# Seven products on three PSUM banks, a down projection that finishes token tile by token tile, and new homes for two kinds of tiles

## The chip, the cores and the metric

The kernel runs on one core of one Trainium2 chip. The metric is the device time of one execution in microseconds (us), as the median of several runs. TensorE (PE) does the matmuls, VectorE (DVE), ScalarE (ACT) and GpSimd (POOL) do the elementwise work, and SyncE (SP) issues every DMA of this kernel, all on one queue, in program order.

## The reference

One layer of a hybrid decoder on 2048 tokens of width 1024, in fp32: a norm, an input projection with three mixers (two gated linear attentions and a linear recurrence), an output projection with a residual, and then a gated feed-forward part with a final norm. The change touches only the feed-forward part, whose inner width is 2688, 21 channels of 128 (`NFF`):

```
h = rmsnorm(x, norm_ffn[l])
gate = causal_dwconv(h @ ffn_w_gate[l], ffn_conv_w[l], ffn_conv_b[l])
x = x + (jax.nn.gelu(gate) * (h @ ffn_w_val[l])) @ ffn_w_down[l]
...
return rmsnorm(x, norm_final)
```

`causal_dwconv` is a convolution over three tokens for each column.

## The kernel before, in words

**fp32 by parts.** Every matmul operand is split into a high and a low fp32r part: ACT copies (`wh`, `gh`: line 100), DVE subtracts (`wl`, `gl`: line 107). A product is then three matmuls, high by high, high by low, low by high (lines 130 to 132 and 992).

**Stages.** Mixers and output projection come first (0 to 975 us); they are not touched. Then two halves of 1024 tokens (`TH`) follow one another, each with an up stage and a down stage: up 0 (975 to 1379 us), down 0 (to 1636), up 1 (to 2027.4), down 1 (to 2261.6), and a tail without matmuls.

**Up** (`up`). For each channel f the gate and the value projection of 1024 tokens (two blocks of 512, `TB`) are computed with seven products of half matrices in place of eight, in Strassen's manner: the weights enter as `x`, `y`, `z`, `w` (sums and differences of the gate's and the value's weights, split by `w_steps`), the tokens as `b1`, `t12`, `t34`, `b22`. A product is 12 matmuls of 512 columns, so a channel is 84. Their sums go to four PSUM banks (`ca` and `cd` of the mm banks, `cb` aux, `cc` sc); ACT and DVE add them up into `gr` (the gate before the convolution), `u` (a partial sum that several results share) and `v` (the value). Then come convolution (`ga`), gelu and `v = ga * v`, which is stored as channel f of `g_ffn` in DRAM (line 1025). Channels use two tile pools in turn, `f_up0` for even and `f_up1` for odd f. The last channel, f = 20, is even.

**Down** (`down`). Token tiles of 128 go in groups, (3, 3, 2) tiles in down 0 and (4, 4) in down 1. A group loads its residuals `xr` (512 KB each, line 1038) and runs over the 21 channels: it loads a row block of `w_down` (`wr`, 512 KB, split into `wh`, `wl`; 3 buffers), loads `graw`, the gated activations of the channel and the group's tokens (192 KB for 3 tiles, 256 KB for 4; 4 buffers, line 1042), splits it into `gh`, `gl` (3 buffers), and adds six matmuls for each tile. After the last channel every tile gets its residual, the final norm and one store of 512 KB. Down 0 also prepares the second half's tokens (`h_steps`: norm, transposes on PE, sums) beside its channels.

**What sets the order.** A scheduler orders the instructions of each engine by priority and by when their buffers come free. Each engine then runs its list strictly in order and stops at a wait, SP too. Pools that follow one another take the same addresses: the down stage's pools `f_g` (`graw`, `gh`, `gl`) and `f_o` (`nfb`, `xr`) lie where `f_up0` and `f_up1` lay. A load into a place must wait until the last reader of that place is done; if that reader was a store, until the store has landed.

**Where the tiles lie** (addresses in a partition). Before: `f_up1` lies 8192 bytes below the top of the up stage's space and so leaves a pad at 191680 to 199872. `graw`'s four buffers fill exactly that pad, which no up tile uses, and all of `f_g` ends at 212160, below `f_up0`. `xr` overlaps the `v` of the last channel.

Of the kernel before, what the change touches and what calls it, by code (L numbers as in the profile page):

```python
# [8 lines left out]
F32 = mybir.dt.float32  # L9
F32R = mybir.dt.float32r  # L10
I32 = mybir.dt.int32
AF = mybir.ActivationFunctionType
ALU = mybir.AluOpType
# [3 lines left out]
P = 128  # L17
D = 1024
KT = D // P
TB = 512  # L20
NTK = TB // P
EPS = 1e-6
# [21 lines left out]
def kernel(ctx: ExitStack, tc: tile.TileContext, x, norm_mix, w_in, hgrn_lower_bounds, hgrn_norm,  # L44
# [10 lines left out]
    def pool_at(stack, nbytes, name, bufs, **kw):  # L55

        stack.enter_context(tc.tile_pool(name="pad_" + name, bufs=1, **kw)).tile([P, nbytes // 4], F32, name="pad")
        return stack.enter_context(tc.tile_pool(name=name, bufs=bufs, **kw))
# [21 lines left out]
    def mm_bank():  # L80
        return bank("mm", 4)

    def aux_bank():
        return bank("aux", 2)

    def sc_bank():
        return bank("sc", 2)
# [16 lines left out]
    def split(raw, hi, lo, e_hi=act, e_lo=vec):  # L104

        copy(e_hi, hi, raw)
        e_lo.tensor_tensor(lo, raw, hi.bitcast(F32), op=ALU.subtract)  # L107
# [20 lines left out]
    def mm3(o, lhs, rhs, first, last):  # L128
        (lh, ll), (rh, rl) = lhs, rhs
        pe.matmul(o, lh, rh, start=first, stop=False)  # L130
        pe.matmul(o, lh, rl, start=False, stop=False)  # L131
        pe.matmul(o, ll, rh, start=False, stop=last)  # L132

    def rms_rstd(src, n):
        junk = junk_t().bitcast(mybir.dt.bfloat16)
        ss = small.tile([P, 1], F32, name="ss")
        act.activation(junk, src, AF.Square, accum_out=ss)
        r = small.tile([P, 1], F32, name="rstd")
        vec.tensor_scalar(r, ss, 1.0 / n, EPS, op0=ALU.mult, op1=ALU.add)  # L139
        pool.tensor_tensor(r, r, half, op=ALU.pow)  # L140
        return r
# [567 lines left out]
    with ExitStack() as cy:  # L709
# [165 lines left out]

        junk_t = lambda: stage.tile([P, TB], F32, name="junk", tag="st")
        hc = cy.enter_context(tc.tile_pool(name="f_hc", bufs=1, reuse_waits="tile"))
        fc = cy.enter_context(tc.tile_pool(name="f_const", bufs=1, reuse_waits="tile"))  # L880
# [95 lines left out]
        def up(hf, H, pools):  # L976

            nextw, steps = w_steps(0)
            for st in steps:
                st()  # L980
            for f in range(NFF):
                W, pool_ = nextw, pools[f % 2]
                if f + 1 < NFF:
                    nextw, steps = w_steps(f + 1)
                else:
                    steps = [lambda: None] * 5

                def prod(o, w, wk, h, hk, first, last):
                    for k in range(KH):
                        lhs, rhs = [a[:, wk + k, :] for a in w], [a[:, hk + k, :] for a in h]  # L990
                        for i, (a, b) in enumerate(((0, 0), (0, 1), (1, 0))):
                            pe.matmul(o, lhs[a], rhs[b], start=first and k == 0 and i == 0, stop=k == KH - 1 and i == 2,  # L992
                                      skip_group_check=True)
                gr = pool_.tile([P, 2 + TH], F32, name="gr")
                ga = pool_.tile([P, TH], F32, name="ga")
                v = pool_.tile([P, TH], F32, name="v")
                u = pool_.tile([P, TB], F32, name="u")
                pool.tensor_copy(gr[:, 0:2], carry[:, f, :])
                steps[0]()
                ca, cb, cd, cc = mm_bank(), aux_bank(), mm_bank(), sc_bank()  # L1000
                prod(ca, W["x"], 0, H["b1"], 0, True, False)
                act.activation(u, ca, AF.Copy)  # L1002
                prod(cb, W["y"], KH, H["t12"], KH, True, True)
                vec.tensor_tensor(u, cb, u, op=ALU.add)
                prod(ca, W["x"], KH, H["b1"], KH, False, True)
                act.activation(gr[:, 2:2 + TB], ca, AF.Copy)
                steps[1]()
                prod(cd, W["y"], 0, H["t12"], 0, True, False)
                vec.tensor_tensor(v[:, TB:], cd, u, op=ALU.add)
                steps[2]()  # L1010
                prod(cc, W["z"], 0, H["t34"], 0, True, False)
                vec.tensor_tensor(v[:, TB:], cc, v[:, TB:], op=ALU.add)
                prod(cd, W["z"], KH, H["b22"], 0, False, True)
                vec.tensor_tensor(gr[:, 2 + TB:], cd, u, op=ALU.add)
                pool.tensor_copy(carry[:, f, :], gr[:, TH:TH + 2])
                act.activation(ga, gr[:, 2:], AF.Identity, bias=pc["fb"][:, f:f + 1], scale=pc["fw2"][:, f:f + 1])
                steps[3]()
                prod(cc, W["w"], 0, H["t34"], KH, False, True)
                vec.tensor_tensor(v[:, :TB], cc, u, op=ALU.add)
                for k in range(2):  # L1020
                    vec.scalar_tensor_tensor(ga, gr[:, k:k + TH], pc[f"fw{k}"][:, f:f + 1], ga,
                                             op0=ALU.mult, op1=ALU.add)
                act.activation(ga, ga, AF.Gelu_apprx_tanh)
                vec.tensor_tensor(v, ga, v, op=ALU.mult)
                sync.dma_start(out=g_ffn[f][:, hf * TH:(hf + 1) * TH], in_=v)
                steps[4]()

        def down(hf, groups, gp, op, nfb, beside=()):

            beside, t0, nst = list(beside), hf * TH // P, sum(1 for _ in groups) * NFF  # L1030
            every, cnt = (nst // (len(beside) + 1) if beside else nst), 0
            for n in groups:
                banks = [[aux_bank(), sc_bank()] if t < 2 else [mm_bank(), mm_bank()] for t in range(n)]
                xr = []
                for t in range(n):
                    xr.append(op.tile([P, D], F32, name="xr", bufs=3))
                    r0 = (t0 + t) * P
                    sync.dma_start(out=xr[t], in_=x2_d[r0 // TB][r0 % TB:r0 % TB + P, :])
                for f in range(NFF):
                    wd = load_w(w_down[f * P:(f + 1) * P, :].rearrange("p (a c) -> p a c", a=2), 2, 512, "ffd")  # L1040
                    graw = gp.tile([P, 4 * P], F32, name="graw", bufs=4)[:, :n * P]
                    sync.dma_start(out=graw, in_=g_ffn[f][:, t0 * P:(t0 + n) * P])
                    g = [gp.tile([P, 4 * P], F32R, name=nm, bufs=3)[:, :n * P] for nm in ("gh", "gl")]
                    split(graw, g[0], g[1])
                    for t in range(n):
                        for h in range(2):
                            mm3(banks[t][h], [a[:, t * P:(t + 1) * P] for a in g], [a[:, h, :] for a in wd],
                                f == 0, f == NFF - 1)
                    cnt += 1
                    if beside and cnt % every == 0:  # L1050
                        beside.pop(0)()
                for t in range(n):
                    y = xr[t]
                    for h in range(2):
                        ysl = y[:, h * 512:(h + 1) * 512]
                        vec.tensor_tensor(ysl, banks[t][h], ysl, op=ALU.add)
                    r = rms_rstd(y, D)
                    vec.scalar_tensor_tensor(y, y, r, nfb, op0=ALU.mult, op1=ALU.mult)
                    sync.dma_start(out=out[(t0 + t) * P:(t0 + t + 1) * P, :], in_=y)
                t0 += n  # L1060
            for st in beside:
                st()
# [5 lines left out]
        for hf in range(NH2):  # L1068
            with ExitStack() as cu:
                upools = [pool_at(cu, 8192, "f_up1", 1, reuse_waits="tile")]  # L1070
                upools.insert(0, cu.enter_context(tc.tile_pool(name="f_up0", bufs=1, reuse_waits="tile")))
                up(hf, H, upools)
            with ExitStack() as cd_:
                gp = cd_.enter_context(tc.tile_pool(name="f_g", bufs=3, reuse_waits="tile"))
                op = cd_.enter_context(tc.tile_pool(name="f_o", bufs=1, reuse_waits="tile"))
                nfb = op.tile([P, D], F32, name="nfb")
                sync.dma_start(out=nfb, in_=norm_final.partition_broadcast(P))
                if hf + 1 < NH2:
                    H, steps = h_steps(hf + 1)
                    down(hf, (3, 3, 2), gp, op, nfb, steps)  # L1080
                else:
                    down(hf, (4, 4), gp, op, nfb)
# [30 lines left out]
```

## Time and profile before

| | |
|---|---|
| median of 3 runs (lowest, highest) | 2273.32 us (2268.23, 2276.04) |
| profiled execution | 2278.91 us |
| its span | 2277.2 us |
| mean granted TensorE clock (share of full speed) | 0.989 |
| PE busy | 2199.7 us (97%) |
| DVE busy, ACT busy, POOL busy | 72%, 42%, 15% |

The span runs from the first to the last instruction of the profiled execution; its own time is 1.7 us longer, and 5.6 us above the median of the runs. PE is busy nearly throughout, so what counts is where it is not: at the joints between stages and in the tail.

### The profile page before, as it was taken

What the parts mean: (1) busy time and instruction counts of PE and PEld (TensorE: products, weight loads), DVE (VectorE), ACT (ScalarE), POOL (GpSimd) and SP (SyncE); (2) the same over time, 40 slices, a digit from 0 to 9 for tenths busy, and PEclk for the clock granted to TensorE, in tenths of its full rate; (3) what the DMA queues carried; (4) which work ended last, traced back from release to release, by engine and by line L of the source; (5) the groups of instructions that cost most, each with busy time, mean ns of one, the idle gap of its engine ahead of it and who ended that gap; (6) DMA issues with size and microseconds to landing.
All of it is one profiled execution on the core that took longest, in us unless ns stands there. A gap on an engine that the chain in (4) does not pass through costs nothing.

```text
span 2277.2 us, 31631 instructions
## 1 busy us (share of the span) xinstructions
PE 2199.7 (97%) x12310; PEld 1806.0 (79%) x12310; DVE 1640.9 (72%) x2264; ACT 951.4 (42%) x1259; POOL 338.0 (15%) x456
## 2 busy tenths in 40 slices
PE   7999999999999999999999999999999999999997
PEld 6887777777667788988888888877888888888785
DVE  7798998989578778777777775657777777763533
ACT  4453535332166276543333344545433333333322
POOL 2231332425233321000000000000000000000000
PEclk9999999999899999999999999999999999999998
DMA  7443422255146546622222237666422222254652
GB/s 260 127 154 96 156 77 65 84 172 181 38 134 209 179 153 189 209 85 82 82 82 84 83 102 233 208 217 233 153 84 84 83 84 83 84 193 140 192 163 80
DMA packets 270676, 307.27 MB, mean 135 GB/s; under 512 B 16947, under 2 KB 225854, under 8 KB 268990
## 3 DMA queue, kind: packets, MB, share of 16 engines
q1 hardware_dynamic: 270526, 305.25, 42.1%
q8 instruction: 96, 1.57, 0.3%
q14 instruction: 54, 0.44, 0.1%
HBM read 243.34 MB, written 61.87 MB: 134 GB/s over the span
## 4 chain that ended last, share of the span: by engine, by line
PE 57%; DVE 6%; DMA 4%; ACT 2%; issue 2%; POOL 1%; SPq 0%; POOLq 0%; DVEq 0%; ACTq 0%
PE mm L992 20%; PE sc L992 10%; PE aux L992 5%; PE sc L131 3%; PE sc L132 3%; PE sc L130 3%; PE mm L131 2%; PE mm L130 2%; PE mm L132 2%; PE aux L132 2%; PE aux L131 2%; PE aux L130 2%; DVE wl L107 1%; DMA x_d<-xr 1%; DMA xt<-x_d 1%
## 5 line engine op out<-in xcount | busy, mean ns | idle before, releaser
L107 DVE TENSOR_TENSOR wl<-wr,wh 128x1024 fp32r<-128x1024 f32 (+2 forms) x289 | 328.5, 1139 | 75.3 <-ACT wh L100 74.4
L100 ACT ACTIVATE wh<-wr 128x1024 fp32r<-128x1024 f32 (+3 forms) x265 | 257.7, 974 | 294.9 <-PE mm L992 131.2
L130 PE MATMUL mm<-hTh,wh 128*128 128x512 f32 x576 | 235.8, 410 | 0.0
L132 PE MATMUL mm<-hTh,wl 128*128 128x512 f32 x576 | 233.3, 405 | 1.5 <-POOL wl L107 1.1
L131 PE MATMUL mm<-hTl,wh 128*128 128x512 f32 x576 | 234.2, 407 | 0.0
L398 POOL TENSOR_TENSOR qc<-Q,X 32x128 f32<-32x128 f32 x224 | 150.8, 673 | 248.7 <-ACT X L384 121.2
L107 DVE TENSOR_TENSOR gl<-graw,gh 128x384 fp32r<-128x384 f32 (+2 forms) x105 | 60.7, 583 | 176.3 <-ACT gh L100 176.2
L100 ACT ACTIVATE wh<-s 128x1024 fp32r<-128x1024 f32 x84 | 89.3, 1063 | 193.0 <-PE mm L992 170.8
L100 ACT ACTIVATE gh<-graw 128x384 fp32r<-128x384 f32 (+2 forms) x105 | 56.8, 545 | 247.5 <-PE mm L131 179.8
L131 PE MATMUL sc<-wl,oh 128*128 128x256 f32 x512 | 147.2, 288 | 2.2 <-DVE wl L107 2.2
L130 PE MATMUL sc<-wh,oh 128*128 128x256 f32 x512 | 146.9, 288 | 1.5 <-DVE xr L828 1.5
L132 PE MATMUL sc<-wh,ol 128*128 128x256 f32 x512 | 145.8, 285 | 0.0
L132 PEld LDWEIGHTS mm<-hTh,wl 128*128 128x128 f32 x576 | 109.8, 191 | 31.0 <-issue 5.1
L140 POOL TENSOR_TENSOR rstd<-rstd,half 128x1 f32<-128x1 f32 x48 | 32.7, 685 | 681.5 <-DVE rstd L139 681.4
L130 PEld LDWEIGHTS mm<-hTh,wh 128*128 128x128 f32 x576 | 109.7, 191 | 29.4 <-issue 7.3
L131 PEld LDWEIGHTS mm<-hTl,wh 128*128 128x128 f32 x576 | 109.6, 190 | 28.1 <-issue 7.3
L992 PE MATMUL mm<-hTh,wh 128*128 128x512 f32 x336 | 130.9, 390 | 0.4 <-ACT u L1002 0.4
L992 PE MATMUL mm<-hTl,wh 128*128 128x512 f32 x336 | 130.8, 389 | 0.0
L992 PE MATMUL mm<-hTh,wl 128*128 128x512 f32 x336 | 130.7, 389 | 0.0
L992 PE MATMUL sc<-t34h,wh 128*128 128x512 f32 x336 | 130.7, 389 | 0.0
L992 PE MATMUL sc<-t34l,wh 128*128 128x512 f32 x336 | 130.7, 389 | 0.0
L992 PE MATMUL sc<-t34h,wl 128*128 128x512 f32 x336 | 130.7, 389 | 0.0
(293 smaller groups left out, 5651.2 us busy)
## 6 DMA issues: line engine op xcount, KB each, us to landing
wr<-in_ffn_w_down_dram SPq DMA_DIRECT2D x105, 512.0 KB
wr<-in_w_in_dram SPq DMA_DIRECT2D x80, 512.0 KB
wr<-in_ffn_w_gate_dram SPq DMA_DIRECT2D x42, 512.0 KB
wr<-in_ffn_w_val_dram SPq DMA_DIRECT2D x42, 512.0 KB
g_ffn<-v SPq DMA_DIRECT2D x42, 512.0 KB
wr<-in_w_out_dram SPq DMA_DIRECT2D x32, 512.0 KB
graw<-g_ffn SPq DMA_DIRECT2D x42, 256.0 KB
xt<-in_x_dram SPq DMA_DIRECT2D x16, 512.0 KB
```

The lines of the kernel that those rows point to most:

```text
L100: act.activation(o, i, AF.Copy)
L107: e_lo.tensor_tensor(lo, raw, hi.bitcast(F32), op=ALU.subtract)
L130: pe.matmul(o, lh, rh, start=first, stop=False)
L131: pe.matmul(o, lh, rl, start=False, stop=False)
L132: pe.matmul(o, ll, rh, start=False, stop=last)
L140: pool.tensor_tensor(r, r, half, op=ALU.pow)
L398: pool.tensor_tensor(qc[p_, h, :].rearrange("p (n s) -> p n s", s=lev), qo[p_, 2], xo[p_, 2], op=ALU.mult)
L992: pe.matmul(o, lhs[a], rhs[b], start=first and k == 0 and i == 0, stop=k == KH - 1 and i == 2, skip_group_check=True)
```

## The change

Up: the products go to three banks, `cx` (mm), `cy_` (sc) and `cz` (aux). A bank goes on being added to after its partial sum was read ("in passing"): `cx` holds four products in a row and is read after the first, the second, the third and the fourth. The tile `u` is gone; ACT makes four copies out of PSUM (before two), DVE three additions (before five).

Down: the last two channels of a group (three in the very last one) are held back, and their matmuls are issued tile by tile, half by half, each half followed by its residual, its sum of squares, and later its own scaling and store of 256 KB. The residuals of tiles 2 and 3 of a group of four live in the pool `xpool` (tag "xt"). The split of `graw` gets a higher priority.

Homes: `f_g` is opened 320 bytes higher, and `f_up0` is 2 KB smaller without `u`. Now `graw` starts at 192000, so its fourth buffer reaches into `f_up1`, `f_g` ends at 212480, over the start of `f_up0`'s `gr` (212192), and `xr` (from 216576) still overlaps the last channel's `v` (220416).

```diff
-                u = pool_.tile([P, TB], F32, name="u")
...
-                ca, cb, cd, cc = mm_bank(), aux_bank(), mm_bank(), sc_bank()
-                prod(ca, W["x"], 0, H["b1"], 0, True, False)
-                act.activation(u, ca, AF.Copy)
-                prod(cb, W["y"], KH, H["t12"], KH, True, True)
-                vec.tensor_tensor(u, cb, u, op=ALU.add)
-                prod(ca, W["x"], KH, H["b1"], KH, False, True)
-                act.activation(gr[:, 2:2 + TB], ca, AF.Copy)
+                g1, g2, v1, v2 = gr[:, 2:2 + TB], gr[:, 2 + TB:], v[:, :TB], v[:, TB:]
+                cx, cy_, cz = mm_bank(), sc_bank(), aux_bank()
+                prod(cx, W["x"], 0, H["b1"], 0, True, False)
+                act.activation(g1, cx, AF.Copy)
+                prod(cy_, W["y"], 0, H["t12"], 0, True, False)
+                act.activation(v2, cy_, AF.Copy)
+                prod(cx, W["y"], KH, H["t12"], KH, False, False)
+                act.activation(g2, cx, AF.Copy)
                 steps[1]()
-                prod(cd, W["y"], 0, H["t12"], 0, True, False)
-                vec.tensor_tensor(v[:, TB:], cd, u, op=ALU.add)
+                prod(cz, W["x"], KH, H["b1"], KH, True, True)
+                vec.tensor_tensor(g1, cz, g1, op=ALU.add)
                 steps[2]()
-                prod(cc, W["z"], 0, H["t34"], 0, True, False)
-                vec.tensor_tensor(v[:, TB:], cc, v[:, TB:], op=ALU.add)
-                prod(cd, W["z"], KH, H["b22"], 0, False, True)
-                vec.tensor_tensor(gr[:, 2 + TB:], cd, u, op=ALU.add)
+                prod(cx, W["z"], 0, H["t34"], 0, False, False)
+                vec.tensor_tensor(v2, cx, v2, op=ALU.add)
+                prod(cy_, W["z"], KH, H["b22"], 0, False, True)
+                vec.tensor_tensor(g2, cy_, g2, op=ALU.add)
...
-                prod(cc, W["w"], 0, H["t34"], KH, False, True)
-                vec.tensor_tensor(v[:, :TB], cc, u, op=ALU.add)
+                prod(cx, W["w"], 0, H["t34"], KH, False, True)
+                act.activation(v1, cx, AF.Copy)
...
-                    xr.append(op.tile([P, D], F32, name="xr", bufs=3))
+                    if n > 3 and t > 1:
+                        xr.append(xpool.tile([P, D], F32, name="xr2", tag="xt"))
+                    else:
+                        xr.append(op.tile([P, D], F32, name="xr", bufs=3))
...
+
+                def mms(t, h, f):
+                    g, wd = ops[f]
+                    mm3(banks[t][h], [a[:, t * P:(t + 1) * P] for a in g], [a[:, h, :] for a in wd],
+                        f == 0, f == NFF - 1)
+
+                late = 3 if (hf, gi) == (NH2 - 1, len(groups) - 1) else 2
...
-                    split(graw, g[0], g[1])
-                    for t in range(n):
-                        for h in range(2):
-                            mm3(banks[t][h], [a[:, t * P:(t + 1) * P] for a in g], [a[:, h, :] for a in wd],
-                                f == 0, f == NFF - 1)
+                    with tc.high_priority(offset=160):
+                        split(graw, g[0], g[1])
+                    ops.append((g, wd))
+                    if f < NFF - late:
+                        for t in range(n):
+                            for h in range(2):
+                                mms(t, h, f)
...
-                        vec.tensor_tensor(ysl, banks[t][h], ysl, op=ALU.add)
-                    r = rms_rstd(y, D)
-                    vec.scalar_tensor_tensor(y, y, r, nfb, op0=ALU.mult, op1=ALU.mult)
-                    sync.dma_start(out=out[(t0 + t) * P:(t0 + t + 1) * P, :], in_=y)
+                        for f in range(NFF - late, NFF):
+                            mms(t, h, f)
+                        ysl = y[:, h * 512:(h + 1) * 512]
+                        vec.tensor_tensor(ysl, banks[t][h], ysl, op=ALU.add)
+                        act.activation(junk_t(), ysl, AF.Square, accum_out=sq[:, h:h + 1])
+                    r = small.tile([P, 1], F32, name="rstd")
+                    vec.tensor_tensor(r, sq[:, 0:1], sq[:, 1:2], op=ALU.add)
+                    vec.tensor_scalar(r, r, 1.0 / D, EPS, op0=ALU.mult, op1=ALU.add)
+                    pool.tensor_tensor(r, r, half, op=ALU.pow)
+                    for h in range(2):
+                        ysl = y[:, h * 512:(h + 1) * 512]
+                        vec.scalar_tensor_tensor(ysl, ysl, r, nfb[:, h * 512:(h + 1) * 512], op0=ALU.mult, op1=ALU.mult)
+                        sync.dma_start(out=out[(t0 + t) * P:(t0 + t + 1) * P, h * 512:(h + 1) * 512], in_=ysl)
...
-                gp = cd_.enter_context(tc.tile_pool(name="f_g", bufs=3, reuse_waits="tile"))
+                gp = pool_at(cd_, 320, "f_g", 3, reuse_waits="tile")
```

Three places show how the order moves. The first is SP's list from up 0 into down 0. `g_ffn_116` and `g_ffn_117` are channels 19 and 20 of the DRAM tensor (`_97` is channel 0), `wr` is a row block of `w_down`. Before:

```order
L1025 DMA g_ffn_116<-v 128x1024
L116 DMA wr<-in_ffn_w_down_dram 128x1024
L1042 DMA graw<-g_ffn_97 128x384
L1042 DMA graw<-g_ffn_98 128x384
L1042 DMA graw<-g_ffn_99 128x384
L1042 DMA graw<-g_ffn_100 128x384
L116 DMA wr<-in_ffn_w_down_dram 128x1024
```

```order
L116 DMA wr<-in_ffn_w_down_dram 128x1024 x2
L1025 DMA g_ffn_117<-v 128x1024
L116 DMA wr<-in_ffn_w_down_dram 128x1024
L1042 DMA graw<-g_ffn_104 128x384
L1077 DMA nfb<-in_norm_final_dram 128x1024
L1038 DMA xr<-x_d_118 128x1024 x3
```

And the same place in the change:

```order
L1026 DMA g_ffn_116<-v 128x1024
L116 DMA wr<-in_ffn_w_down_dram 128x1024 x4
L1026 DMA g_ffn_117<-v 128x1024
L1098 DMA nfb<-in_norm_final_dram 128x1024
L1042 DMA xr<-x_d_118 128x1024 x3
L1053 DMA graw<-g_ffn_97 128x384
L1053 DMA graw<-g_ffn_98 128x384
L1053 DMA graw<-g_ffn_99 128x384
```

The loads of `graw` for channels 0 to 6 stood ahead of the last channel's store; now the first of them stands behind that store, behind `nfb` and behind three residuals. From up 1 into down 1 it is the same with two residuals ahead of the first `graw`, which were three behind it.

The second place is ACT's list over one channel in the middle of up 1. `s` holds the sums of weights that are split for the next channel, `pcol` the convolution's factors. Before:

```order
L1016 ACTIVATE ga<-gr,pcol_400 128x1024
L100 ACTIVATE wh<-s_14786 128x1024
L1002 ACTIVATE u<-mm 128x512
L1023 ACTIVATE ga<-ga 128x1024
L100 ACTIVATE wh<-wr 128x512
L1006 ACTIVATE gr<-mm 128x512
L100 ACTIVATE wh<-wr 128x1024
L100 ACTIVATE wh<-s_14884 128x1024
```

And in the change:

```order
L1017 ACTIVATE ga<-gr,pcol_400 128x1024
L100 ACTIVATE wh<-s_14916 128x1024
L1020 ACTIVATE v<-mm 128x512
L1003 ACTIVATE gr<-mm 128x512
L1024 ACTIVATE ga<-ga 128x1024
L1005 ACTIVATE v<-sc 128x512
L100 ACTIVATE wh<-wr 128x512
L1007 ACTIVATE gr<-mm 128x512
L100 ACTIVATE wh<-wr 128x1024
```

Two copies of 512 columns come in (lines 1005 and 1020); the copy of line 1007, which the fifth product waits for, stands behind the split of the `w` weights.

The third place is the end of DVE's list, the last tiles of down 1. `aux`, `sc` and `mm` are PSUM banks. Before:

```order
L139 TENSOR_SCALAR rstd<-ss 128x1
L1058 SCALAR_TENSOR_TENSOR xr<-xr,rstd,nfb 128x1024
L1056 TENSOR_TENSOR xr<-mm,xr 128x512 x2
L139 TENSOR_SCALAR rstd<-ss 128x1
L1058 SCALAR_TENSOR_TENSOR xr<-xr,rstd,nfb 128x1024
```

And in the change (`xr_18138` is the last tile's residual):

```order
L1079 SCALAR_TENSOR_TENSOR xr_18136<-xr_18136,rstd,nfb 128x512 x2
L1071 TENSOR_TENSOR xr_18138<-mm,xr_18138 128x512 x2
L1074 TENSOR_TENSOR rstd<-sq_18923 128x1
L1075 TENSOR_SCALAR rstd<-rstd 128x1
L1079 SCALAR_TENSOR_TENSOR xr_18138<-xr_18138,rstd,nfb 128x512 x2
```

Before, each of the four tiles had its additions after the last channel's matmuls of all four; now a tile is finished while PE works on the next one, and SP's list has the last tile's residual long before and no load between the last stores.

## Rows read from the trace of the kernel before

**Rows 1.** The page, part 1: busy us (share of the span), instructions.

```profile
PE 2199.7 (97%) x12310; PEld 1806.0 (79%) x12310; DVE 1640.9 (72%) x2264; ACT 951.4 (42%) x1259; POOL 338.0 (15%) x456
```

**Rows 2.** Windows by stage: length, busy PE, PEld, DVE, ACT, POOL, clock, DMA, GB/s.

```profile
975.00:1379.04 404.04, 404.04 (x1802) 334.95 (x1800) 291.35 (x348) 156.56 (x178) 20.11 (x44) 1.00 0.28 89
1379.04:1636.00 256.96, 250.69 (x1114) 204.26 (x1113) 169.09 (x223) 125.04 (x190) 12.20 (x16) 0.99 0.66 215
...
2027.41:2261.61 234.20, 233.22 (x1009) 189.59 (x1007) 94.34 (x108) 70.53 (x92) 3.12 (x5) 1.00 0.50 155
2261.61:2277.20 15.59, 0.00 (x0) 0.00 (x0) 6.03 (x10) 2.30 (x4) 1.65 (x3) 0.60 0.46 168
```

**Rows 3.** Waits of PE from 975 us on: us in total, times, longest.

```profile
PE aux L130 <- ACT gh L100: 2.8, 1, 2.8
PE aux L132 <- DVE gl L107: 2.0, 1, 2.0
...
PE mm L130 <- DVE xr L1056: 1.0, 1, 1.0
```

**Rows 4.** Timeline of SP, 1355 to 1400 us: start, length, the issues merged.

```profile
1370.58 1.85 SPq L1042 DMA_DIRECT2D graw<-g_ffn  x4
...
1385.34 0.33 SPq L1025 DMA_DIRECT2D g_ffn<-v  x1
...
1387.83 2.02 SPq L1038 DMA_DIRECT2D xr<-x_d  x3
1390.06 4.40 SPq L116 DMA_DIRECT2D wr<-in_ffn_w_down_dram  x2
```

**Rows 5.** Timeline of PE and of ACT where up 0 ends.

```profile
1379.04 0.39 PE L130 MATMUL aux<-wh,gh 128*128 128x512 f32 x1
...
1374.67 1.49 ACT L100 ACTIVATE gh<-graw 128x384 fp32r<-128x384 f32 x3 [2.71 <-DMA graw<-g_ffn]
```

**Rows 6.** Timeline of DVE at the same place, up to the last channel's product.

```profile
1379.95 0.68 DVE L1019 TENSOR_TENSOR v<-sc,u 128x512 f32<-128x512 f32 x1
1380.55 1.21 DVE L107 TENSOR_TENSOR wl<-wr,wh 128x1024 fp32r<-128x1024 f32 x1
...
1384.09 1.23 DVE L1024 TENSOR_TENSOR v<-ga,v 128x1024 f32<-128x1024 f32 x1 [1.13 <-ACT ga L1023]
```

**Rows 7.** The chain that ended last, in order of time: start, us, what.

```profile
1566.20 5.18 DMA out_dram<-xr
...
2261.65 2.67 DMA out_dram<-xr
2264.33 4.55 DMA xr<-x_d
...
2272.39 1.28 DVE xr L1058
```

**Rows 8.** DMA, 1380 to 1400 us, in 40 slices of 0.5 us.

```profile
GB/s 205 442 328 33 0 115 188 369 311 25 25 16 311 410 369 139 147 319 364 278 179 245 270 328 344 385 410 434 426 426 401 410 442 418 426 401 403 313 242 124
```

**Rows 9.** Windows around down 0's last group, and in the mixers (columns: rows 2).

```profile
1583.00:1589.00 6.00, 3.26 (x13) 2.40 (x14) 6.00 (x11) 3.48 (x8) 0.00 (x0) 1.00 0.61 206
1589.00:1592.40 3.40, 3.40 (x10) 2.65 (x9) 2.32 (x4) 1.12 (x2) 0.00 (x0) 0.50 0.50 151
1592.40:1595.80 3.40, 3.40 (x16) 2.74 (x16) 1.59 (x2) 1.37 (x2) 0.00 (x0) 0.99 0.58 184
...
595.50:599.00 3.50, 3.50 (x10) 1.83 (x10) 0.00 (x0) 0.00 (x0) 0.00 (x0) 0.50 0.00 0
```

**Rows 10.** Timeline of the tail: the last tile's residual, squares, and a power.

```profile
2263.90 0.55 POOL L140 TENSOR_TENSOR rstd<-rstd,half 128x1 f32<-128x1 f32 x1 [1.53 <-DVE rstd L139]
...
2269.00 1.29 DVE L1056 TENSOR_TENSOR xr<-mm,xr 128x512 f32<-128x512 f32 x2 [3.23 <-DMA xr<-x_d]
2270.32 1.06 ACT L137 ACTIVATE junk<-xr 128x1024 bf16<-128x1024 f32 x1 [6.86 <-DVE xr L1056]
```

**Rows 11.** Timeline of ACT in one channel of up 1.

```profile
1769.03 0.63 ACT L100 ACTIVATE wh<-wr 128x512 fp32r<-128x512 f32 x1 [3.19 <-PE mm L992]
1769.57 0.58 ACT L1006 ACTIVATE gr<-mm 128x512 f32<-128x512 f32 x1
...
1783.83 1.06 ACT L1023 ACTIVATE ga<-ga 128x1024 f32<-128x1024 f32 x1 [0.42 <-DVE ga L1021]
```

More of the change, by code (lines that the diff above doesn't have):

```diff
@@ L1031, in down @@
             every, cnt = (nst // (len(beside) + 1) if beside else nst), 0
-            for n in groups:
+            for gi, n in enumerate(groups):
                 banks = [[aux_bank(), sc_bank()] if t < 2 else [mm_bank(), mm_bank()] for t in range(n)]
-                xr = []
+                xr, ops = [], []
                 for t in range(n):
-                    xr.append(op.tile([P, D], F32, name="xr", bufs=3))
+                    if n > 3 and t > 1:
+                        xr.append(xpool.tile([P, D], F32, name="xr2", tag="xt"))
+                    else:
+                        xr.append(op.tile([P, D], F32, name="xr", bufs=3))
                     r0 = (t0 + t) * P
                     sync.dma_start(out=xr[t], in_=x2_d[r0 // TB][r0 % TB:r0 % TB + P, :])
+                def mms(t, h, f):
[3 more added lines that the diff above has]
+                late = 3 if (hf, gi) == (NH2 - 1, len(groups) - 1) else 2
                 for f in range(NFF):
@@ L1052, in down @@
                 for t in range(n):
-                    y = xr[t]
+                    y, sq = xr[t], op.tile([P, 2], F32, name="sq2", bufs=4)
+                    for h in range(2):
[8 more added lines that the diff above has]
+                    pool.tensor_tensor(r, r, half, op=ALU.pow)
                     for h in range(2):
                         ysl = y[:, h * 512:(h + 1) * 512]
-                        vec.tensor_tensor(ysl, banks[t][h], ysl, op=ALU.add)
-                    r = rms_rstd(y, D)
-                    vec.scalar_tensor_tensor(y, y, r, nfb, op0=ALU.mult, op1=ALU.mult)
-                    sync.dma_start(out=out[(t0 + t) * P:(t0 + t + 1) * P, :], in_=y)
+                        vec.scalar_tensor_tensor(ysl, ysl, r, nfb[:, h * 512:(h + 1) * 512], op0=ALU.mult, op1=ALU.mult)
+                        sync.dma_start(out=out[(t0 + t) * P:(t0 + t + 1) * P, h * 512:(h + 1) * 512], in_=ysl)
                 t0 += n
```

## The prediction

> **What bounds the kernel now.** First the page's busy times: PE works 2199.7 of 2277.2 us [rows 1]. A change that takes work off DVE or ACT gains only where PE waits for it. So the next view is the table by stage [rows 2]: in up 0 PE is busy in all 404.04 us of 404.04, and there is nothing to gain; down 0 has 6.27 us without PE (256.96 less 250.69), down 1 has 0.98, and the tail has 15.59 with no matmul at all. The list of PE's waits names those in the stages [rows 3]: 2.8 us for a `gh` and 2.0 for a `gl` where down 0's last group begins, 1.0 for a residual's addition between down 1's groups. The tail is a chain through one buffer [rows 7]: a store at 2261.65, whose landing (2.67 us) lets the last tile's residual be loaded (4.55), then its norm, and a store that ends the span. That is all that can be won: some 22 us. The other side is what now hides: at both joints from up to down PE does not wait at all. The first down matmul starts at 1379.04, where up ends, because its `gh` was split at 1374.67 from a `graw` that was issued at 1370.58, while up still ran [rows 4, 5].
>
> **Up stages: 0.** DVE loses two additions of 0.68, ACT gains two copies of 0.58 [rows 6, 11], and PE has the same 84 matmuls a channel. Its 21 x 84 = 1764 matmuls stand 404.04 / 1764 = 0.229 us apart, so a product is 2.75. PE could begin to wait because product five (from 11.0 us of a channel on) must find `cx` read. ACT gets there as follows: product three ends at 8.25, then comes the split of the `w` weights (0.63), then the copy (0.58) [rows 11], so 9.5: 1.5 us to spare. Product seven waits for a DVE addition of 0.68 behind product five, with a whole product's 2.75 us between. So 0 each, hidden by those products; if the cover were gone, see the rivals.
>
> **The joints from up to down: +28.** This is where I differ from what the diff seems to say. SP runs its list in order, and with the new places the first `graw` stands behind the last channel's store, `nfb` and the residuals. The first residual lies where that store still reads `v`, so SP stops there until the store has landed, and all `graw` loads stop with it. Counted from the end of up's matmuls (E):
> - Store issued. Before it was E + 6.3 (1385.34 less 1379.04) [rows 4, 5]. The change takes an addition of 0.68 (now ACT's) and a split of 1.21 from between the two convolution steps; the other split lies beside gelu, in the 1.13 us that DVE now waits [rows 6]. So E + 4.4.
> - Landed. The uncontended store of the tail took 2.67, a contended one 5.18 [rows 7]. At the joint of before the three residuals took 2.02 us to issue, about 0.9 more than three issues need (an issue is 0.33 to 0.38), and one of them waited for the same store; that puts its landing near 1388.7, 3.3 us after its issue [rows 4]. I take 3.3: E + 7.7.
> - Three residuals of 512 KB, then `graw`. A 192 KB load took 4.1 us from issue to its split with one 512 KB load just ahead [rows 4, 5]; at the 0.43 MB/us that the queue reaches [rows 8] those 0.7 MB are 1.7 us, so 2.4 is fixed. Now 1.7 MB lie from the first residual on: 2.2 + 4.0 = 6.2 (the fixed part less what overlaps). E + 13.9. The lower bound takes the residuals as if they cost issue time alone (1.1 + 4.1), the upper 4.55 fixed and contended (E + 17).
> - Split of `gh`, 0.5 [rows 5]: PE starts at E + 14.5, bounds 11 and 18.
> - At the second joint two residuals stand ahead and `graw` has 256 KB: 1.0 us less, 13.5.
>
> Sum 28, bounds 21 to 33. Behind the stopped SP stand the weight loads of the channels that follow, too, but four row blocks are already in.
>
> [...]
>
> **The clock after a joint: +3.2.** In down 0's last group PE had 2.75 and 1.97 us of idle time; then the granted clock was 0.50 for 3.4 us, which held 10 matmuls where the next 3.4 us held 16 [rows 9]: 6 matmuls of 0.229 or half of 3.4 us, so 1.4 to 1.7 us lost. In a longer stretch of the mixers the clock stayed at half without any idle time [rows 9], so one restart may cost more; I take 1.6 twice, with an upper end of 7 in all. The Trainium skill, "TensorE: Matmul & The Clock Gate", Part 1, says that an idle array comes back at 1.2 GHz, half of 2.4; the trace agrees with 0.50.
>
> **Starts of groups: +2.5 new, -6.3 and -1.0 gone.** Before, down 0's last group began with 2.75 + 1.97 us of waiting for `gh` and `gl`, behind a chain of transposes' splits on ACT and DVE, and then 1.6 us of slow clock. The `graw` splits now have priority, and the tile-by-tile end gives 3 tiles x 12 matmuls in which they can run: -6.3 (0 if the transposes' splits still stand ahead). The 1.0 us between down 1's groups [rows 3] waited for a residual behind a store; tiles 2 and 3 now have buffers of their own: -1.0. But held-back channels keep two of three `wh`/`wl` buffers until the last tile's matmuls, so the next group's second row block is split late: a split is 1.06 on ACT and 1.21 on DVE against the 18 or so matmuls of the first channel (4.1 us). I estimate 0.8, 1.2 and 0.5 us at three starts: +2.5, bounds 0 and 6.
>
> **The tail: -8.7.** The last residual is there in advance. After PE: half an addition pair (1.29 / 2 = 0.65), half a square (0.6), its accumulator and two small DVE steps (0.5), the power (0.55) [rows 10], two half scalings (1.28 [rows 7]), and the store. The last one of before took from 2273.67 (2272.39 + 1.28) to the span's end at 2277.2, 3.5 us; half as many bytes save at most 0.6. 0.65 + 0.6 + 0.5 + 0.55 + 1.28 + 3.2 = 6.8, and 0.1 for the steps between: 6.9 in place of 15.59 [rows 2]. Bounds 6.1 and 8.1.
>
> **Sum.** 28 + 3.2 + 2.5 - 6.3 - 1.0 - 8.7 = +17.7 us. The profiled execution of 2278.91 us would become 2296.6; it lies 5.6 us above the median, so the median of 2273.32 becomes 2291.
>
> **The rivals.** *The joints are shorter, and the time does not change.* If residuals and `graw` run beside each other, the joint is 10.5 us: the store's issue at 4.4, 2.7 for its landing, and 3.4 to the first split. Two such joints, no slow clock, the group stalls gone and the tail at its best give 21 - 7.3 - 9.5 = +4, 2277. The point at which joints decide: gains of 16.0 less 2.5 new are 13.5, so 6.7 us a joint break even. Below that it would be faster; for that the first `graw` would have to land within 6.2 us of E, and its queue's head is issued only at 4.4. It could happen only if the chip's order differed from the list. *The joints hide wholly*, because nothing of the down stage is late: -16 + 2.5, 2260. For it speaks that before `graw` came 4 us early; against it the order of SP. *Reads in passing stop PE.* If the split of `w`'s weights came one product later, the copy behind it would end 1.1 us after product five should start; 42 channels x 1.1 = 46 us, plus 17.7: 2337. Against it stands 1.5 us of slack.
>
> A change of under 0.3% (6.8 us) can hardly be told from none here. Forecast (2281 to 2304): 0.80. Joints shorter, no change that can be measured: 0.09. Hidden joints, faster: 0.06. Reads stop PE: 0.05. Slower is the forecast and the last, 0.85. The range is that of the forecast with its bounds: from 21 + 3.2 - 7.3 - 9.5 = +7.4 (2281) to 33 + 5 + 4 - 4 - 7.5 = +30.5 (2304), where the smaller terms are not all at their upper ends at once.
>
> **What would show it.** In the profile after: PE waits twice for `ACT gh` at about 13 to 15 us, each behind `DMA graw<-g_ffn`; `g_ffn`'s store stands ahead of `xr` and `graw` on SP at both joints; the clock is 0.50 behind both. PE's up stages have no wait in them at the new copies (line 1007). The last matmul is followed by about 7 us. I would be wrong if the first down matmul again followed up's last one directly, or if PE waited in each channel.

## The result, and the profile after

The changed kernel takes 2297.80 us in the median of 6 runs (2294.13 to 2301.39), the kernel before 2275.37 in the median of 5. A sixth run of the kernel before took 6760.68 us and is left out. The ratio is 1.0106, with a 95% interval of 1.0088 to 1.0124. It is slower by 22.4 us, where 17.7 were forecast (2291, range 2281 to 2304). The profiled execution has a span of 2294.7 us, 17.5 more than before; its mixers happened to end 4.0 us earlier (the first up matmul stands at 974.9 in place of 978.9 us), so of the span the part that the change touches grew by 21.5.

The stages of the changed kernel, in the columns of [rows 2], cut at PE's first matmul of each stage and at its last. The rows of before in [rows 2] are cut elsewhere (its up 0 begins at 978.9 and not at 975, its up 1 at 1626.8 and not at 1636), so the lengths of its stages can't be set against these; only the time without PE can.

```profile
975.00:1374.97 399.97, 399.97 (x1765) 330.89 (x1764) 259.96 (x297) 174.50 (x215) 27.50 (x44) 1.00 0.27 86
1374.97:1633.63 258.66, 239.75 (x1073) 196.77 (x1073) 161.56 (x225) 125.32 (x202) 7.37 (x12) 0.97 0.67 214
1633.63:2036.62 402.99, 400.83 (x1765) 330.76 (x1763) 260.92 (x301) 172.95 (x216) 27.15 (x44) 1.00 0.28 88
2036.62:2286.28 249.66, 231.04 (x1009) 190.29 (x1008) 100.11 (x126) 75.42 (x112) 6.48 (x7) 0.97 0.50 154
2286.28:2294.70 8.42, 0.16 (x1) 0.00 (x0) 3.91 (x8) 1.33 (x4) 0.55 (x1) 0.74 0.32 125
```

Up 0 is full of matmuls, as it was. The two down stages are not: 18.9 and 18.6 us without PE. The last row is cut 0.16 us before the last matmul ends (2286.44); from there the tail is 8.3 us long, before 15.59 [rows 2]. PE's waits from 960 us on, answering [rows 3]:

```profile
PE aux L130 <- ACT gh L100: 34.7, 2, 17.7
PE mm L910 <- DVE xt L151: 1.2, 1, 1.2
PE sc L993 <- DVE wl L107: 1.1, 1, 1.1
PE mm L993 <- ACT gr L1003: 1.0, 1, 1.0
PE mm L130 <- DVE xr L1071: 0.9, 1, 0.9
PE mm L910 <- ACT wh L100: 0.7, 1, 0.7
PE aux L132 <- DVE gl L107: 0.4, 1, 0.4
PE aux L131 <- DVE wl L107: 0.3, 1, 0.3
```

Two waits make nearly all of it. Here is the first, on SP (answering [rows 4]), ACT and PE; up's last matmul ends at 1374.97:

```profile
1366.53 11.87 SPq L116 DMA_DIRECT2D wr<-in_ffn_w_down_dram  x4
1379.28 0.33 SPq L1026 DMA_DIRECT2D g_ffn<-v  x1
1379.77 0.33 SPq L1098 DMA_DIRECT2D nfb<-in_norm_final_dram  x1
1383.21 1.28 SPq L1042 DMA_DIRECT2D xr<-x_d  x3
1384.53 15.04 SPq L1053 DMA_DIRECT2D graw<-g_ffn  x8
...
1391.41 1.44 ACT L100 ACTIVATE gh<-graw 128x384 fp32r<-128x384 f32 x3 [13.42 <-DMA graw<-g_ffn]
...
1391.99 0.79 PE L130 MATMUL aux<-wh,gh 128*128 128x512 f32 x1 [17.02 <-ACT gh L100]
```

Read from the top: the store is issued 4.3 us after up's end, the first residual 3.9 us later, the first `graw` at 9.6 us; it lands 6.9 us on, and PE has waited 17.02 us. The chain of the second joint shows the same (start, us, what; up ends at 2036.62):

```profile
2041.00 4.60 DMA g_ffn<-v
2045.62 0.33 SPq L1042
...
2046.47 7.10 DMA graw<-g_ffn
```

Behind the first joint, where PE had been idle for 17 us, the granted clock was at half and then came back (windows, columns of [rows 2]), as in [rows 9]:

```profile
1391.90:1395.30 3.40, 3.31 (x8) 2.64 (x9) 1.51 (x3) 0.95 (x3) 0.00 (x0) 0.50 0.46 137
1395.30:1398.70 3.40, 3.40 (x15) 2.73 (x14) 0.04 (x1) 0.60 (x2) 0.00 (x0) 0.88 0.14 47
```

One thing in the trace was not expected. Down matmuls stand closer than before, with the same granted clock of 1.00. Here are the first and the last of 58 consecutive ones in down 1 of the kernel before, and then the same of the changed kernel, where 59 fit in:

```profile
2099.74 0.39 PE L131 MATMUL sc<-wl,gh 128*128 128x512 f32 x1
...
2112.79 0.39 PE L131 MATMUL mm<-wl,gh 128*128 128x512 f32 x1
```

```profile
2099.64 0.39 PE L132 MATMUL mm<-wh,gl 128*128 128x512 f32 x1
...
2112.79 0.39 PE L130 MATMUL sc<-wh,gh 128*128 128x512 f32 x1
```

13.05 / 57 = 0.2289 us before, 13.15 / 58 = 0.2267 after. In the last groups of both down stages of before it was 0.2333. Here are the first and the last of 58 in the last group of down 1 (13.30 / 57):

```profile
2199.62 0.40 PE L132 MATMUL mm<-wh,gl 128*128 128x512 f32 x1
...
2212.92 0.40 PE L132 MATMUL aux<-wh,gl 128*128 128x512 f32 x1
```

After the change it is 0.2267 in all groups. Up 0, whose operands did not move, has 1764 matmuls in 400.1 us before and in 400.0 after, 0.2268 us for one.

### The profile page after: what moved, and what is told of

It is laid out like the page before. It is cut to its first block, busy times and chain, and to the rows that moved or that the text cites. A ratio compares the mean times of both kernels' runs of the same rounds, so it can differ in the third digit from the quotient of the medians.

```text
span 2294.7 us, 31743 instructions
## 1 busy us (share of the span) xinstructions
PE 2191.8 (96%) x12310; PEld 1805.5 (79%) x12310; DVE 1591.0 (69%) x2212; ACT 997.4 (43%) x1375; POOL 352.8 (15%) x456
## 5 line engine op out<-in xcount | busy, mean ns | idle before, releaser
L130 PE MATMUL mm<-hTh,wh 128*128 128x512 f32 x576 | 234.1, 407 | 0.0
L132 PE MATMUL mm<-hTh,wl 128*128 128x512 f32 x576 | 231.5, 402 | 1.5 <-POOL wl L107 1.1
L131 PE MATMUL mm<-hTl,wh 128*128 128x512 f32 x576 | 232.2, 403 | 0.0
L993 PE MATMUL mm<-t34h,wh 128*128 128x512 f32 x336 | 131.0, 390 | 0.0
L993 PE MATMUL mm<-t34h,wl 128*128 128x512 f32 x336 | 130.8, 389 | 0.0
L993 PE MATMUL mm<-t34l,wh 128*128 128x512 f32 x336 | 130.8, 389 | 0.0
L130 PE MATMUL aux<-wh,gh 128*128 128x512 f32 x210 | 83.7, 398 | 34.7 <-ACT gh L100 34.7
L107 DVE TENSOR_TENSOR wl<-s,wh 128x1024 fp32r<-128x1024 f32 x84 | 102.6, 1222 | 8.9 <-ACT wh L100 8.9
L1022 DVE SCALAR_TENSOR_TENSOR ga<-gr,pcol,ga 128x1024 f32<-128x1024 f32 x84 | 107.8, 1283 | 0.1
L131 PEld LDWEIGHTS sc<-wl,oh 128*128 128x128 f32 x512 | 98.4, 192 | 5.9 <-DVE wl L107 2.9
```

## The experiments

Each kernel's time is given with its ratio to the kernel before on the same chip. The chips differ between the runs, so two changed kernels are compared by these ratios.

**The old home of the gated tiles.**

```diff
-                gp = pool_at(cd_, 320, "f_g", 3, reuse_waits="tile")
+                gp = cd_.enter_context(tc.tile_pool(name="f_g", bufs=3, reuse_waits="tile"))
```

> The change, with the pool of gated tiles back at its old address (no 320 bytes), all else as changed. Theory (the moved pool overlaps the last channel's gr by 288 bytes, and that puts the graw loads behind the last store): both joints return to no wait, 34.7 us of waits and some 3.5 us of slow clock go; but the matmuls of the down stages stand 0.2289 us apart again in place of 0.2267, 2090 x 0.0022 = 4.6 us: about 2264 us. Rival one (the tile-by-tile end or the raised priority of the splits makes the joints late): the joints stay at 17 us, about 2298. Rival two (the matmul spacing comes from something else than the address): spacing stays 0.2267, about 2260.

Measured: 2262.66 us, ratio 0.9952 (0.9936 to 0.9968). The joints have no wait; the longest of PE's is 1.2 us. The down matmuls stand 0.2289 us apart (58 in 13.05), in the last groups too, where the kernel before had 0.2333. Here is down 1's last group, 60 matmuls:

```profile
2199.28 0.39 PE L131 MATMUL mm<-wl,gh 128*128 128x512 f32 x1
...
2212.78 0.39 PE L130 MATMUL sc<-wh,gh 128*128 128x512 f32 x1
```

So the late joints come from the new place, not from the tile-by-tile end or the priority, and the step from 0.2289 to 0.2267 comes from it too.

**The new home, without the overlap.**

```diff
-                upools = [pool_at(cu, 8192, "f_up1", 1, reuse_waits="tile")]
+                upools = [pool_at(cu, 8512, "f_up1", 1, reuse_waits="tile")]
```

> The change with both up pools 320 bytes higher as well, so that the gated tiles keep their new address and no longer overlap gr of the last channel. Theory: no wait at the joints and 0.2267 us between down matmuls: 2297.8 - 34.7 - 3.5 = about 2260 us. Rival one (late end or priority makes the joints late): about 2298.

Measured: 2256.94 us, ratio 0.9937 (0.9917 to 0.9957). Against the changed kernel's 1.0106 that is 1.7% or some 38 us less, by 320 bytes. From the first up matmul to the end of the span, which leaves the mixers out, it is 1280.4 us in place of 1319.8 (before: 1298.3). PE's waits of this kernel, from 950 us on, where the first row of the changed kernel's list is gone and the rest stands:

```profile
PE mm L910 <- DVE xt L151: 1.2, 1, 1.2
PE sc L993 <- DVE wl L107: 1.1, 1, 1.1
PE mm L993 <- ACT gr L1003: 1.0, 1, 1.0
PE mm L130 <- DVE xr L1071: 0.9, 1, 0.9
```

The matmuls keep their 0.2267 us. This version is faster than both kernels, by 0.6% than the one before.

**The kernel before, with nothing but addresses changed.**

```diff
-                upools = [pool_at(cu, 8192, "f_up1", 1, reuse_waits="tile")]
+                upools = [pool_at(cu, 8512, "f_up1", 1, reuse_waits="tile")]
...
-                gp = cd_.enter_context(tc.tile_pool(name="f_g", bufs=3, reuse_waits="tile"))
+                gp = pool_at(cd_, 320, "f_g", 3, reuse_waits="tile")
```

> The kernel before with nothing but addresses changed: gated tiles and up pools 320 bytes higher, in the same order. Theory (the address of gh and gl sets the spacing of the down matmuls): 0.2267 us in place of 0.2289 (about 1400 matmuls) and of 0.2333 (about 730): 3.1 + 4.8 = 8 us less than before, about 2267.5. Rival (the spacing comes from the new order of work or from fewer DVE and ACT conflicts): spacing as before, 0.2289 and 0.2333, about 2275.

Measured: 2266.45 us, ratio 0.9975 (0.9965 to 0.9985), 5.5 us less than before, and 59 matmuls in 13.14 us, 0.2266. So the new address gives 0.2267 with the old order of work too. At the old address the order does matter: there the kernel before has 0.2333 in its last groups, and the first experiment, with the new order, 0.2289. The interval of the gain, 3.4 to 8.0 us, just reaches the 8 us that the spacing alone would give. PE's waits from up 0 on changed little in sum: two of [rows 3] became longer here (3.1 for `gh`, 1.9 for `xr`), that for `gl` shorter.

**Residuals behind the gated tiles' loads.**

```diff
-                    r0 = (t0 + t) * P
-                    sync.dma_start(out=xr[t], in_=x2_d[r0 // TB][r0 % TB:r0 % TB + P, :])
+                def load_xr():
+                    for t in range(n):
+                        r0 = (t0 + t) * P
+                        sync.dma_start(out=xr[t], in_=x2_d[r0 // TB][r0 % TB:r0 % TB + P, :])
...
+                    if f == 6:
+                        load_xr()
```

> The change with the residual loads of a group written behind its sixth channel, homes as changed; graw's loads then stand ahead of the residuals, but still behind the last channel's store and nfb. Theory: of the 17 us at a joint the residuals ahead (and the store's landing that they wait for) make about 7: PE starts some 10.5 us after up's last matmul, both joints 21, and the time falls by about 14 to 2284 us. Rival (the first graw's landing is late for the store and nfb in the DMA queue, not for the residuals): joints stay near 17, about 2298.

Measured: 2285.50 us, ratio 1.0072 (1.0046 to 1.0098). PE waits 12.72 and 14.03 us in place of 17.02 and 17.72. The SP rows and the splits of this kernel at the first joint, where up ends at 1370.3:

```profile
1374.59 0.33 SPq L1026 DMA_DIRECT2D g_ffn<-v  x1
1375.09 0.33 SPq L1103 DMA_DIRECT2D nfb<-in_norm_final_dram  x1
1375.46 2.54 SPq L1058 DMA_DIRECT2D graw<-g_ffn  x4
...
1382.43 1.50 ACT L100 ACTIVATE gh<-graw 128x384 fp32r<-128x384 f32 x3 [9.12 <-DMA graw<-g_ffn]
```

The first `graw` is issued 5.2 us after up's end and not at 9.6, so the store's landing and the residuals' issues cost 4.4 us, as the chain of issues says. But it still takes 7.0 us to land (8.0 at the second joint), with no residual ahead of it. From the store's issue to the split the queue was busy nearly all the time (columns of [rows 2]: DMA share 0.90, at 296 GB/s, which makes 2.3 MB):

```profile
1374.59:1382.43 7.84, 0.00 (x0) 0.00 (x0) 0.00 (x0) 0.00 (x0) 0.00 (x0) 0.50 0.90 296
```

The store and `nfb` are 1.0 MB of it and the four `graw` loads issued together 0.8. So the expectation's rival, that the first `graw` is late for what the queue carries besides the residuals, is true of a part. The time is as expected; the waits are 2 to 3.5 us longer than the 10.5 that I had put.

**Which overlap.**

```diff
-                upools.insert(0, cu.enter_context(tc.tile_pool(name="f_up0", bufs=1, reuse_waits="tile")))
+                upools.insert(0, pool_at(cu, 320, "f_up0", 1, reuse_waits="tile"))
```

> The change with only f_up0 320 bytes higher: the gated tiles' last buffer no longer overlaps gr of the last channel by 288 bytes, but graw's fourth buffer still overlaps gr of the channel before. Theory (the 288 bytes under the last channel's gr are the whole cause): no wait at the joints, about 2258 us as with both up pools moved (2256.9). Rival (the overlap of graw's own buffer with f_up1 holds the loads back): joints stay near 17 us, about 2298.

Measured: 2258.88 us, ratio 0.9951 (0.9935 to 0.9968), no wait at the joints. So `graw`'s overlap with `f_up1`, which stays here, is not the cause. The edit takes two things off the last channel's tiles, though: `gl`'s last buffer no longer reaches 288 bytes into `gr`, and by the addresses the first residual (to 220672) no longer reaches 256 bytes into `v` (from 220416, now from 220736). The run does not separate them. With the residuals behind the sixth channel, above, `graw` still stood behind the store; that leaves the 288 bytes under `gr` as the cause of the order.

**The up stage alone.** The kernel before with the three-bank products and without `u`, the first part of the change's diff.

> The kernel before with the three-bank up stage alone; down stages and the place of the gated tiles as before. Theory (PE has no wait in the up stages to lose, before or after): PE's list of waits shows none in the channels but those at up 1's start (0.4 before, 2.2 in the changed kernel), the time is that of before, 2272 to 2276 us. Rival (reads in passing stop PE in each channel): 1.1 us x 42, about 2318. Rival (fewer DVE additions help somewhere): 2265 or less.

Measured: 2275.73 us, ratio 1.0019 (1.0002 to 1.0035). PE's list has no wait in the channels except at up 1's start (1.0 and 0.2 us). Neither a gain nor the stop in each channel; a loss of up to 0.35% is within the interval.

**Fewer loads behind the first.**

```diff
-                    graw = gp.tile([P, 4 * P], F32, name="graw", bufs=4)[:, :n * P]
+                    graw = gp.tile([P, 4 * P], F32, name="graw", bufs=2)[:, :n * P]
...
-                gp = pool_at(cd_, 320, "f_g", 3, reuse_waits="tile")
+                gp = pool_at(cd_, 320 + 4096, "f_g", 3, reuse_waits="tile")
```

> The change with two buffers for graw in place of four, all other addresses as changed. Theory (loads issued one behind the other run side by side, so the first graw lands with those behind it): with one in place of three graw loads issued behind the first, 0.39 and 0.52 MB less are in flight, and the first graw lands 0.9 and 1.2 us sooner after its issue than 6.9 and 7.1: both joints together about 32.5 us in place of 34.7; about 2296, if two buffers are enough elsewhere. Rival (loads land in order of issue): 6.9 and 7.1 stay.

Measured: 2299.49 us, ratio 1.0125 (1.0110 to 1.0140). The chain of the second joint has a landing of 5.70 us in place of 7.10:

```profile
2045.46 4.92 DMA g_ffn<-v
...
2051.24 5.70 DMA graw<-g_ffn
```

At the first joint it did not move (issue at 1383.79, split at 1390.80, 7.0 us). That decides it for neither side, and two buffers cost waits of their own (four for `gh` in place of two). What the 7 us are made of stays open in part: the queue was busy, as above, but which load delays which is not shown.

**The additions first.** The kernel of the second experiment ("The new home, without the overlap"), with

```diff
+                        with tc.high_priority(offset=60):
+                            vec.tensor_tensor(ysl, banks[t][h], ysl, op=ALU.add)
+                            act.activation(junk_t(), ysl, AF.Square, accum_out=sq[:, h:h + 1])
```

> The change with both up pools 320 bytes higher (2256.9 us) and the residuals' additions and squares ahead of the scaling of the tile before. Theory (in the tail the last tile's second addition stands 1.0 us behind the scaling of the tile before): the tail after the last matmul is 7.6 us in place of 8.3, the time about 2256; nothing else changes.

Measured: 2258.87 us, ratio 0.9943 (0.9922 to 0.9964). A miss: DVE's list became scaling, addition, scaling, addition, so the last addition still begins 1.3 us after the last matmul's end (2249.35 and 2248.05), and the tail is 8.2 us, where it was 8.3.

**Other addresses for the gated tiles**, one run each: the kernel of the second experiment with 576, 448 and 384 bytes in place of 320 (and 8768, 8640 and 8576 in place of 8512).

> The change without the overlap, gated tiles at 256 bytes past a multiple of 512 (before: 192 past one; changed kernel: on one). Read here is only the distance between down matmuls in down 1. Theory (a 128-column slice of gh or gl is 512 bytes a partition, and costs time when it straddles a 512-byte boundary): about 0.2289 us. Rival (256 bytes are enough): 0.2267.

> The same with 128 bytes past a multiple of 512. Theory (any straddling of 512 bytes): about 0.2289 us between down matmuls. Rival (128 is enough, or 192 alone is bad): 0.2267.

> The same with 64 bytes past a multiple of 512, the remainder that 192 has over 128. Theory (any straddling of 512 bytes): about 0.2289 us. Rival one (a multiple of 64 that is no multiple of 128 is bad, 128 and 256 are good): 0.2289 here and 0.2267 there. Rival two (192 alone): 0.2267.

Measured: 2264.57, 2267.01 and 2267.65 us, beside 2273.04 for the kernel before. From single runs only the distances are read. First and last down matmul of a stretch of 59 with 256 bytes, and of 57 with 64:

```profile
2099.69 0.39 PE L132 MATMUL mm<-wh,gl 128*128 128x512 f32 x1
...
2112.84 0.39 PE L130 MATMUL aux<-wh,gh 128*128 128x512 f32 x1
```

```profile
2099.84 0.39 PE L132 MATMUL mm<-wh,gl 128*128 128x512 f32 x1
...
2112.91 0.39 PE L131 MATMUL aux<-wl,gh 128*128 128x512 f32 x1
```

That is 13.15 / 58 = 0.2267 and 13.07 / 56 = 0.2334; with 128 bytes it is 0.2325 here (58 in 13.25). My theory, that only a multiple of 512 will do, is wrong: 256 is as good. Of the remainders tried, 0 and 256 are fast, 64, 128 and 192 are slow.

## Why the prediction was right, point by point

- **The joints: the step held, its size was 34.7 and not 28.** That is above my upper bound of 33, which was put too low: the two joints' own upper ends, 18 and 17, add up to 35. The store left at E + 4.3 (4.4 forecast). Its landing took 3.9 and 4.6 us, not 3.3. The larger error is the term from the first residual to the first `graw`: 8.2 us at the first joint, not 6.2, and 8.0 at the second, not 5.2. I had reckoned with the 0.43 MB/us that the queue reached in [rows 8]; from the first residual's issue to the first split it moved 0.318 MB/us:

```profile
1383.21:1391.41 8.20, 0.00 (x0) 0.00 (x0) 0.00 (x0) 0.00 (x0) 0.00 (x0) 0.50 0.92 318
```

That is 2.6 MB, where I had counted 1.7, and the first three `graw` loads were there at once (ACT splits three in a row). That the loads behind the first share its time fits the second joint with two buffers, and not the first.
- **That the residuals are the cause was half right.** They and the store cost some 4 us a joint (17.02 to 12.72, 17.72 to 14.03). The rest is that the `graw` loads stand behind the store's issue at all, and this comes from 288 shared bytes, with which a pool of 20 KB was put behind the last channel.
- **The clock: 3.2 forecast.** From the windows half of 3.4 us and a further 0.12 of 3.4, 2.1 at the first joint; the second had 0.50 and 0.91 over the same lengths, 2.0. Sum 4.1.
- **Up stages: 0, right**, by the trace and by the up stage alone. The 0.229 us between matmuls was misread: the 404.04 us of [rows 2] hold 1802 matmuls, 38 of them of the output projection. By 0.2268 a product is 2.72 us and not 2.75; the slack that I gave for the reads barely changes with it. Only up 1's start was missed: 1.1 and 1.0 us of waits, 0.4 before.
- **Starts of groups.** The stalls of 4.7 us went, the wait of 1.0 us became 0.9 at another addition, and the new ones are 0.7 us, not 2.5.
- **The tail: 8.3 us, not 6.9.** The term that was missing is the scaling of the tile before: it keeps DVE until 2287.18, while the last matmul ends at 2286.44, and only then come the two additions. 0.74 of waiting and 1.28 for the pair stand where I had 0.65:

```profile
2285.85 1.42 DVE L1079 SCALAR_TENSOR_TENSOR xr<-xr,rstd,nfb 128x512 f32<-128x512 f32 x2 [0.73 <-POOL rstd L1076]
...
2286.05 0.39 PE L132 MATMUL mm<-wh,gl 128*128 128x512 f32 x1
...
2287.18 1.28 DVE L1071 TENSOR_TENSOR xr<-mm,xr 128x512 f32<-128x512 f32 x2
```

- **What the forecast did not have: some 6 us of gain from the address of `gh` and `gl`.** I costed the 320 bytes only by what they overlap. It is 5.5 us by the kernel before at new addresses, and 5.7 between the first two experiments' medians. The other terms as measured are 34.7 + 4.1 + 0.7 + 1.7 - 6.3 - 0.1 - 7.3 = 27.5 (the 1.7 is up 1's start, the 6.3 the group's stalls with the slow clock behind them). The measured 21.5 is 6.0 less, which is this gain. So it was luck that the total came within 4 us of the forecast: an effect that I did not know of hid that joints, clock and tail were reckoned too short. With 27.5 the time would have been 2301, still within the range.

The rivals: the joints did not shrink, and PE did not stop in each channel. Without the joints the change is about what its parts promise: 15.0 us faster than before (2256.94 against the 2271.97 measured beside it).

## What to carry to other kernels

When tiles move, list what lies under them before and after: one tile that reaches a few hundred bytes into a buffer that is used until the end of a stage can push a whole row of loads behind that stage's last store, and the instruction order shows it without a run. A load that needs a late buffer should not stand ahead of the loads that the next matmul needs, on a queue that runs in order. And look at the distance between matmuls, not only at their waits: a busy engine can still be 1 to 3% slow.

## What the runs showed of the hardware

The place of the stationary operand sets the distance between fp32r matmuls of 512 columns, at a granted clock of 1.00: 0.2267 us with the 128-column slices at 0 or 256 bytes past a multiple of 512, 0.2289 to 0.2334 at 64, 128 and 192. `graw`, `nfb` and `xr` moved along with `gh` and `gl`, but among what PE reads only these two moved. What in the chip makes the difference was not shown, nor whether other remainders are fast. Why one and the same address (192) gives 0.2289 in some stretches and 0.2333 in others was not found: in the kernel before the step comes where the waits of [rows 3] stand, at down 0's last group and between down 1's groups, but the up stage alone, with a wait of 1.4 us at the same place, stayed at 0.2289 behind it.
